# A transformer block on one core: its two inputs also handed over feature-major, and the first loads put in another order

## The chip, the core and the metric

The kernel runs on one core of a Trainium2 chip, in one launch. A core has five engines that work side by side and wait for each other through semaphores: TensorE (PE; its weight loads are listed as PEld), VectorE (DVE), ScalarE (ACT), GpSimd (POOL) and SyncE (SP). SP does nothing but issue DMA transfers here; ACT and POOL can issue them too, each from its own queue, in the order in which the instructions stand on that engine. The metric is the device time of one execution in microseconds (us). The kernel before takes 927.66 us (median of three runs, 927.59 to 928.44).

## What is computed

One block of a hybrid encoder, in float32, for 512 tokens `x` (512 x 1024) and 256 memory tokens `mem` (256 x 1024). Cut to what the change touches:

```python
h = rms_norm(x, g_mix)                      # x * rsqrt(mean(x*x) + eps) * g_mix, row by row
z = h @ w_in                                # every branch reads a part of z
mem_n = rms_norm(mem, mem_g)
kv = mem_n @ w_kv                           # keys: first 512 columns, values: the other 512
# attention of z's query part over k, v; latent attention; mLSTM; gated merge; SwiGLU; final norm
```

The rest of the block (three branches, their gated merge, the output projection, the feed-forward part and the final norm) is some 880 of the 925 us and has the same code before and after.

## The kernel before

**Matmuls in three terms.** A float32 product is made of two parts of each operand: `split` (line 83) writes `hi`, a rounded copy (made by ACT, line 85 or 88), and `lo`, the rest (made by DVE, line 86 or 89). `mm3` (line 101) then issues three matmuls for each pair: hi*hi, hi*lo and lo*hi (lines 104 to 106). So each weight tile costs a load (SP, line 94), one ACT and one DVE pass of 1024 columns (`wload`), and only then matmuls. `raw` has two buffers, `w_hi` and `w_lo` three.

**The head.** TensorE multiplies over features, so it needs `x` and `mem` with features on the partitions, and they arrive with tokens on the partitions. Four stages follow each other, each in one loop:

1. `mem` (two tiles of 128 tokens, four loads of half a tile) is turned by 16 transposes on PE (line 365), and split with the gain `mg_t` from PSUM into `mt_hi`, `mt_lo`.
2. The norm factors: ACT squares each row tile and sums it (lines 372 and 377), DVE makes mean + eps (`n_v`, line 113), POOL the power -0.5 (`n_r`, line 115). `x`'s four tiles are multiplied by their factor in place (line 380 or 382). `mem`'s factor `rm` is applied later.
3. The values: four chunks `c` of `w_vm`, each 12 matmuls of 512 columns into the two banks `vps`, which are scaled with `rm` when they are split into `v_hi`, `v_lo`.
4. The keys, for `h` in 0 to 3: eight transposes of `x` (line 404), split with the gain `gx_t` into two feature tiles of `h_hi`, `h_lo` (lines 88 and 89); then one weight tile of `w_kt` with 24 matmuls of 256 columns into a bank of `pg` (two banks). DVE reads that bank once (`kf`, line 410, times `rbc`, the factors of `mem` as a row), which frees it for the key after the next.

`prepare` (line 263) loads five small constants by SP (line 265) at the end of the head in the code, and POOL zeroes a few tiles. After the head come the tiles of `w_in` (`z_tile`, line 205): 24 matmuls of 512 columns each over all of `h_hi` and `h_lo`; the first two are queries of the memory attention.

**What sets the order.** The code is not run in the order in which it is written. A scheduler in the compiler, with a model of the engines, puts each engine's instructions into one fixed list; a change at the start moves rows in all of it. On the chip each engine then takes its list strictly in order. DMA completions are counted on eight semaphores that SP's and ACT's transfers share in turn, so a transfer is issued only when the eighth transfer before it has landed; that wait stands on the issuing engine, in its list.

**Farther on.** `finish_pair` (line 621) ends a pair of mLSTM heads: four transposes of `hn` (line 633), then `tho` on DVE (line 634) and `ob_hi` on ACT (line 88). `latent_units` (line 696) squares two z tiles on ACT (`csq`, `sq`, line 723), adds them on DVE (line 709) and sums the rows by four small matmuls with `ones` (line 714).

Of the kernel before, what the change touches and what calls it, by code (L numbers as in the profile page):

```python
# [19 lines left out]
P = 128  # L20
S = 512
NT = S // P
D = 1024
KD = D // P
DFF = 2816
NF = DFF // P
MEM = 256
NMT = MEM // P
# [29 lines left out]


@with_exitstack  # L60
def block_kernel(ctx, tc, x, mem, pos, inv, g_mix, mem_g, g_ffn, g_final, g_q, g_kv, gate_bias,
                 g_head, conv_w, w_zt, w_kt, w_vm, w_uq, w_uk, w_uv, w_qk,
                 w_br, w_out, w_fg, w_fu, w_fd, out):
    nc = tc.nc
    mm = nc.tensor.matmul
    V = nc.vector
# [111 lines left out]
    with ExitStack() as mix:  # L178
# [146 lines left out]
        with tc.tile_pool(name="xp", bufs=1) as xp:  # L325
            mt_hi = xp.tile([P, KD, MEM], F32R, name="mt_hi")
            mt_lo = xp.tile([P, KD, MEM], F32R, name="mt_lo")
            gx_t = xp.tile([P, KD], F32, name="gx_t")
            mg_t = xp.tile([P, KD], F32, name="mg_t")

            def load_x(src, t, eng):
                xt = xp.tile([P, D], F32, name="xt", tag="xt", bufs=6)
                eng.dma_start(out=xt, in_=src[t * P:(t + 1) * P, :])
                return xt

            nc.scalar.dma_start(out=mg_t, in_=mem_g)
            nc.scalar.dma_start(out=gx_t, in_=g_mix)
            mxs = [xp.tile([P, D], F32, name="xt", tag="xt", bufs=6) for _ in range(NMT)]

            def load_mem(half):  # L340
                cols = slice(half * 512, (half + 1) * 512)
                for t in range(NMT):
                    nc.sync.dma_start(out=mxs[t][:, cols], in_=mem[t * P:(t + 1) * P, cols])
# [5 lines left out]
            raws, xs, wvs = {}, [], {}  # L349
            load_mem(0)  # L350
            load_mem(1)
            wvs[0] = wload(w_vm[0], pieces=2)
            wvs[1] = wload(w_vm[1])
            load_v(2)
            xs.append(load_x(x, 0, nc.sync))
            load_v(3)
            xs.append(load_x(x, 1, nc.sync))
            xs.append(load_x(x, 2, nc.sync))
            xs.append(load_x(x, 3, nc.sync))
            for k0 in range(0, KD, 2):  # L360
                tp = bank(ptp if k0 % 4 else pg)
                for k in range(2):
                    for t in range(NMT):
                        c0 = k * MEM + t * P
                        nc.tensor.transpose(tp[:, c0:c0 + P], mxs[t][:, (k0 + k) * P:(k0 + k + 1) * P], ident)
                for k in range(2):
                    split(mt_hi[:, k0 + k], mt_lo[:, k0 + k], tp[:, k * MEM:(k + 1) * MEM], scale=mg_t[:, k0 + k:k0 + k + 1])
            rm = xp.tile([P, NMT], F32, name="rm")
            for t in range(NMT):
                junk = xp.tile([P, D], F32, name="junk", tag="junk", bufs=1)  # L370
                ss = xp.tile([P, 1], F32, name="ss", tag="ss", bufs=2)
                A.activation(junk, mxs[t], AF.Square, accum_out=ss)
                V.tensor_copy(rm[:, t:t + 1], rsqrt_mean(xp, ss, 1, D, "n"))
            for t in range(NT):
                junk = xp.tile([P, D], F32, name="junk", tag="junk", bufs=1)
                ss = xp.tile([P, 1], F32, name="ss", tag="ss", bufs=2)
                A.activation(junk, xs[t], AF.Square, accum_out=ss)
                r = rsqrt_mean(xp, ss, 1, D, "n")
                if t % 2:
                    A.activation(xs[t], xs[t], AF.Copy, scale=r)  # L380
                else:
                    V.tensor_scalar(out=xs[t], in0=xs[t], scalar1=r, scalar2=None, op0=ALU.mult)
            vps = [bank(psc) for _ in range(NMT)]
            for c in range(4):
                wh, wl = wvs[c] if c < 2 else wload(w_vm[c], raw=raws[c])
# [5 lines left out]
            rbc = xp.tile([P, MEM], F32, name="rbc")  # L391
            tp = bank(pg)
            for t in range(NMT):
                rb = xp.tile([P, P], F32, name="rb", tag="rb", bufs=2)
                V.tensor_scalar(out=rb, in0=ones, scalar1=rm[:, t:t + 1], scalar2=None, op0=ALU.mult)
                nc.tensor.transpose(tp[:, t * P:(t + 1) * P], rb, ident)
            A.activation(rbc, tp[:, :MEM], AF.Copy)
            for t in range(NMT):
                split(v_hi[:, t], v_lo[:, t], vps[t], scale=rm[:, t:t + 1])
            for h in range(4):  # L400
                for k in (2 * h, 2 * h + 1):
                    tp = bank(ptp)
                    for t in range(NT):
# [4 lines left out]
                gemm_t(ps[:, :MEM], wh, wl, KD, mt_hi, mt_lo)  # L408
                kf = xp.tile([P, MEM], F32, name="kf", tag="kf", bufs=2)
                V.tensor_tensor(out=kf, in0=ps[:, :MEM], in1=rbc, op=ALU.mult)  # L410
                split(k_hi[:, h], k_lo[:, h], kf)
            prepare()

        def gate_chain():
            fp = mq
# [732 lines left out]
```

## Time and profile before

| what | us |
|---|---|
| median of three runs | 927.66 |
| the profiled execution | 925.3 |
| its span, first to last instruction | 923.4 |
| PE busy in the span | 905.1 |
| DVE busy in the span | 636.1 |
| ACT busy in the span | 509.2 |

The profile is of one execution. Times in its rows are from the start of its span; the span lies 1.9 us inside the execution's own time, and that execution was 2.4 us under the median of the timed runs. Busy time of PE is pipelined: a matmul's row lasts longer than the step to the next one, so the steps between starts are what a stream of matmuls costs.

### The profile page before, as it was taken

To read this page: it belongs to the slowest core of one execution; us is meant where nothing else is said; L and a number is where in the kernel's file an instruction comes from. 1 tells how busy PE (TensorE), PEld (TensorE's weight loads), DVE (VectorE), ACT (ScalarE), POOL (GpSimd) and SP (SyncE) were. 2 spreads that over 40 slices of the span, in tenths; PEclk is the share of its full clock that TensorE was granted. 3 is DMA by queue.
4 is the path that set the end of the run, shared out by engine and by line. 5 is a ranking of instruction groups with operands and counts; after the bars stand their busy time and mean duration, and the time that the engine had idled before them with its cause. 6 is when DMAs were issued, how large, how long until landed. Compare 5 with 4: busy or idle time off the path is not lost.

```text
span 923.4 us, 13931 instructions
## 1 busy us (share of the span) xinstructions
PE 905.1 (98%) x5282; PEld 787.7 (85%) x5282; DVE 636.1 (69%) x1088; ACT 509.2 (55%) x896; POOL 85.2 (9%) x139
## 2 busy tenths in 40 slices
PE   7998999999999999999999999999999999999997
PEld 5987787878888788888888879999999999988886
DVE  5768968888684856677553855989898988354323
ACT  8565676686653456677574445545454545244222
POOL 2001002121111101001000500000000000000200
PEclk9999999999999999999999999999999999999999
DMA  7421244434432122121224250423434431365322
GB/s 274 161 75 47 77 133 125 157 121 140 140 111 92 50 86 83 40 87 60 78 69 160 90 191 17 160 93 125 149 115 127 159 115 69 105 225 162 106 76 91
DMA packets 36675, 104.82 MB, mean 114 GB/s; under 512 B 5169, under 2 KB 7537, under 8 KB 36609
## 3 DMA queue, kind: packets, MB, share of 16 engines
q1 hardware_dynamic: 34560, 99.65, 32.4%
q0 software_dynamic: 1184, 3.24, 1.0%
q10 hardware_dynamic: 864, 1.06, 0.3%
q8 instruction: 41, 0.67, 0.3%
q14 instruction: 26, 0.21, 0.1%
HBM read 97.55 MB, written 6.37 MB: 113 GB/s over the span
## 4 chain that ended last, share of the span: by engine, by line
PE 90%; DVE 4%; DMA 2%; ACT 1%; issue 1%; POOL 0%; POOLq 0%; DVEq 0%; SPq 0%; ACTq 0%
PE pg L104 17%; PE pg L106 17%; PE pg L105 17%; PE po L104 7%; PE po L106 7%; PE po L105 7%; PE psc L104 2%; PE psc L105 2%; PE psc L106 2%; PE ptp L818 2%; DVE w_lo L86 1%; PE ppv L588 1%; PE ppv L587 1%; DMA raw<-w_out_d 1%; PE ppv L586 1%
## 5 line engine op out<-in xcount | busy, mean ns | idle before, releaser
L86 DVE TENSOR_TENSOR w_lo<-raw,w_hi 128x1024 fp32r<-128x1024 f32 (+3 forms) x112 | 126.0, 1127 | 92.4 <-ACT w_hi L85 90.7
L104 PE MATMUL pg<-h_hi,w_hi 128*128 128x512 f32 (+1 forms) x476 | 175.2, 369 | 0.8 <-DVE q_lo L89 0.6
L105 PE MATMUL pg<-h_lo,w_hi 128*128 128x512 f32 (+1 forms) x476 | 175.6, 369 | 0.0
L106 PE MATMUL pg<-h_hi,w_lo 128*128 128x512 f32 (+1 forms) x476 | 175.1, 368 | 0.3 <-DVE w_lo L86 0.3
L85 ACT ACTIVATE w_hi<-raw 128x1024 fp32r<-128x1024 f32 (+3 forms) x112 | 107.0, 958 | 104.4 <-PE pg L105 57.2
L104 PEld LDWEIGHTS pg<-h_hi,w_hi 128*128 128x128 f32 x476 | 89.6, 188 | 15.4 <-DVE q_lo L89 0.8
L106 PEld LDWEIGHTS pg<-h_hi,w_lo 128*128 128x128 f32 x476 | 89.5, 188 | 14.8 <-DVE w_lo L86 0.7
L105 PEld LDWEIGHTS pg<-h_lo,w_hi 128*128 128x128 f32 x476 | 89.5, 188 | 13.7
L571 ACT ACTIVATE e<-e,ccol 128x512 f32<-128x512 f32 (+3 forms) x64 | 32.3, 554 | 28.2 <-DMA e<-a_dr 27.6
L1073 DVE TENSOR_REDUCE nm<-psc 128x1 f32<-128x512 f32 (+1 forms) x48 | 27.7, 596 | 19.9 <-PE psc L106 19.5
L576 DVE TENSOR_TENSOR e<-e,psc 128x512 f32<-128x512 f32 (+3 forms) x64 | 29.1, 482 | 17.5 <-POOL e L574 14.6
L1076 ACT ACTIVATE pn<-psc,nm 128x512 f32<-128x512 f32 (+1 forms) x48 | 29.4, 614 | 17.6 <-DVE nm L1073 17.6
L85 ACT ACTIVATE w_hi<-rawab 128x1024 fp32r<-128x1024 f32 x19 | 20.1, 1059 | 29.0 <-PE pg L105 17.4
L574 POOL TENSOR_SCALAR_AFFINE_SELECT e<-e 128x128 f32<-128x128 f32 x64 | 24.0, 384 | 121.5 <-ACT e L571 110.2
L104 PE MATMUL po<-h_hi,w_hi 128*128 128x256 f32 (+1 forms) x116 | 33.8, 291 | 1.4 <-ACT w_hi L85 1.4
L86 DVE TENSOR_TENSOR w_lo<-rawab,w_hi 128x1024 fp32r<-128x1024 f32 x19 | 23.2, 1222 | 16.1 <-ACT w_hi L85 16.0
L1079 ACT ACTIVATE pn<-pn,rs 128x512 f32<-128x512 f32 (+1 forms) x48 | 29.8, 651 | 7.7 <-DVE rs L1078 7.5
L105 PE MATMUL po<-h_lo,w_hi 128*128 128x256 f32 (+1 forms) x116 | 33.7, 290 | 0.0
L106 PE MATMUL po<-h_hi,w_lo 128*128 128x256 f32 (+1 forms) x116 | 33.6, 290 | 0.0
L86 DVE TENSOR_TENSOR s_lo<-e,s_hi 128x640 fp32r<-128x640 f32 x32 | 26.1, 825 | 4.3 <-ACT s_hi L85 2.6
L105 PE MATMUL po<-w_lo,act_hi 128*128 128x512 f32 (+1 forms) x74 | 27.4, 375 | 0.0
L85 ACT ACTIVATE w_hi<-s 128x1024 fp32r<-128x1024 f32 x19 | 20.1, 1059 | 12.9 <-PE pg L105 9.9
(511 smaller groups left out, 2565.3 us busy)
## 6 DMA issues: line engine op xcount, KB each, us to landing
raw<-w_zt_d SPq DMA_DIRECT2D x46, 512.0 KB, 3.4
raw<-w_fd_d SPq DMA_DIRECT2D x22, 512.0 KB, 3.4
e<-a_dr SPq DMA_DIRECT2D x32, 320.0 KB, 3.4
rawab<-w_fg_d SPq DMA_DIRECT2D x19, 512.0 KB, 3.8
rawab<-w_fu_d SPq DMA_DIRECT2D x19, 512.0 KB, 4.7
raw<-w_br_d SPq DMA_DIRECT2D x12, 512.0 KB, 3.5
raw<-w_out_d SPq DMA_DIRECT2D x8, 512.0 KB, 3.6
act_dr<-u SPq DMA_DIRECT2D x16, 256.0 KB, 3.9
```

The costliest lines, as they stand in the source:

```text
L85: A.activation(hi, src, AF.Copy)
L86: V.tensor_tensor(out=lo, in0=src, in1=hi, op=ALU.subtract)
L104: mm(ps, wh, ah, start=start and i == 0, stop=False, skip_group_check=more)
L105: mm(ps, wh, al, start=False, stop=False, skip_group_check=more)
L106: mm(ps, wl, ah, start=False, stop=stop and i == n - 1, skip_group_check=more)
L571: A.activation(e[:, c0:c0 + n], e[:, c0:c0 + n], AF.Exp, bias=ccol[:, j, d, row:row + 1])
L574: nc.gpsimd.affine_select(out=dg, in_=dg, pattern=[[sgn, P]], compare_op=ALU.is_ge, fill=0.0, base=0, channel_multiplier=-sgn)
L576: V.tensor_tensor(out=e[:, c0:c0 + n], in0=e[:, c0:c0 + n], in1=sc[:, t0:t0 + n], op=ALU.mult)
L818: nc.tensor.transpose(tp[:, c * 256 + q * P:c * 256 + (q + 1) * P], pn[q][:, (kt + c) * P:(kt + c + 1) * P], ident)
L1073: nc.vector.tensor_reduce(out=nm, in_=sc, axis=AX.X, op=ALU.max, negate=True)
L1076: nc.scalar.activation(pn, sc, AF.Exp, bias=nm, accum_out=sm)
L1079: nc.scalar.activation(pn, pn, AF.Copy, scale=rs)
```

## The change

The launch hands over two more arrays: `x_t` and `mem_t`, the same numbers with features on the partitions (128 x 8 x 512 and 128 x 8 x 256). `mem_t` is loaded in four pieces of two feature tiles (`mc`) and split from SBUF; `x_t` in four pieces (`xc`). No transposes of `x` and `mem` are left. The row-major `x` and `mem` are still loaded, as whole tiles, for the norm factors alone, and share a ring of six buffers with `x_t`. The factors of `x` are no longer applied to rows: `as_rows` spreads each over a 128 x 128 tile (`rb`, DVE) and transposes that on PE into a bank, and eight new DVE operations (line 397 of the changed kernel) multiply each feature tile by its gain and that bank, in place, before it is split. `mem`'s two factors are made after the values' matmuls instead of before. `prepare` moves to the front, and its five small loads from SP to ACT.

```diff
             for dst, src in ((bias_t, gate_bias), (convw, conv_w), (gh2, g_head), (gq_t, g_q), (gkv_t, g_kv)):
-                nc.sync.dma_start(out=dst, in_=src)
+                nc.scalar.dma_start(out=dst, in_=src)
...
+            prepare()
+
+            def load_mt(k0):
+                mc = xp.tile([P, 2, MEM], F32, name="mc", tag="mc", bufs=4)
+                nc.sync.dma_start(out=mc, in_=mem_t[:, k0:k0 + 2])
+                for k in range(2):
+                    split(mt_hi[:, k0 + k], mt_lo[:, k0 + k], mc[:, k], scale=mg_t[:, k0 + k:k0 + k + 1])
...
+            def load_xt(k0):
+                xc = xp.tile([P, D], F32, name="xc", tag="xt", bufs=6).rearrange("p (k c) -> p k c", k=2)
+                nc.sync.dma_start(out=xc, in_=x_t[:, k0:k0 + 2])
+                return xc
...
+            def as_rows(ps, rs):
+                for t, r in enumerate(rs):
+                    rb = xp.tile([P, P], F32, name="rb", tag="rb", bufs=2)
+                    V.tensor_scalar(out=rb, in0=ones, scalar1=r, scalar2=None, op0=ALU.mult)
+                    nc.tensor.transpose(ps[:, t * P:(t + 1) * P], rb, ident)
...
+            load_mt(0)
             wvs[0] = wload(w_vm[0], pieces=2)
+            load_mt(2)
+            rx = [factor(x, 0)]
             wvs[1] = wload(w_vm[1])
+            load_mt(4)
+            rx.append(factor(x, 1))
             load_v(2)
...
+            load_mt(6)
+            rx.append(factor(x, 2))
+            rx.append(factor(x, 3))
+            xcs = [load_xt(0), load_xt(2)]
...
+            rm = [factor(mem, t) for t in range(NMT)]
+            rbx = bank(ptp)
+            as_rows(rbx, rx)
             for h in range(4):
+                xc = xcs.pop(0)
+                if h < 2:
+                    xcs.append(load_xt(2 * h + 4))
                 for k in (2 * h, 2 * h + 1):
-                    tp = bank(ptp)
-                    for t in range(NT):
-                        nc.tensor.transpose(tp[:, t * P:(t + 1) * P], xs[t][:, k * P:(k + 1) * P], ident)
-                    split(h_hi[:, k], h_lo[:, k], tp, scale=gx_t[:, k:k + 1])
+                    hf = xc[:, k % 2]
+                    V.scalar_tensor_tensor(out=hf, in0=hf, scalar=gx_t[:, k:k + 1], in1=rbx, op0=ALU.mult, op1=ALU.mult)
+                    split(h_hi[:, k], h_lo[:, k], hf)
```

**ACT's list, its start.** The names are the small constants and the parts of `mem`; DMAHW0 to DMAHW7 are the eight semaphores of transfers. Before:

```order
L336 DMA mg_t<-mem_g_d 128x8
L337 DMA gx_t<-g_mix_d 128x8
L88 ACT_TABLE_LOAD [waits DMAHW0_49]
L88 ACTIVATE mt_hi<-pg,mg_t 128x256 [waits PE_49]
L372 ACTIVATE junk,ss<-xt 128x1024 [waits DMAHW4_49,DMAHW1_49]
L88 ACTIVATE mt_hi<-ptp,mg_t 128x256 [waits PE_49]
```

And now:

```order
L330 DMA mg_t<-mem_g_d 128x8
L331 DMA gx_t<-g_mix_d 128x8
L265 DMA bias_t<-gate_bias_d 128x1
L265 DMA convw<-conv_w_d 128x20
L265 DMA gh_94<-g_head_d 128x4 [waits DMAHW1_49]
L265 DMA gq_t<-g_q_d 128x3 [waits DMAHW3_49]
L265 DMA gkv_t<-g_kv_d 128x2 [waits DMAHW5_49]
L88 ACT_TABLE_LOAD
L88 ACTIVATE mt_hi<-mc,mg_t 128x256 [waits DMAHW0_49]
L88 ACTIVATE mt_hi<-mc,mg_t 128x256
L85 ACTIVATE w_hi<-raw 128x512 [waits DMAHW2_49]
L85 ACTIVATE w_hi<-raw 128x512
```

Five DMA issues now stand ahead of ACT's first computing instruction, and the last three of them wait for transfers: semaphore 1 is that of the first `mc`, 3 that of `gx_t`, 5 that of `bias_t`.

**DVE's list, where values end and keys begin** (`w_lo<-raw` are weight tiles, here of `w_vm`, `w_kt` and `z` in turn; `xc` the new in-place products; `kf` the read of a key's bank). Before, from the split of the last chunk of values' weights and of the first key's:

```order
L86 TENSOR_TENSOR w_lo<-raw,w_hi 128x1024 x2
L89 SCALAR_TENSOR_TENSOR v_lo<-psc,rm,v_hi 128x512 x2
L89 SCALAR_TENSOR_TENSOR h_lo<-ptp,gx_t,h_hi 128x512 x2
L86 TENSOR_TENSOR w_lo<-raw,w_hi 128x1024
L410 TENSOR_TENSOR kf<-pg,rbc 128x256
L86 TENSOR_TENSOR w_lo<-raw,w_hi 128x1024
L86 TENSOR_TENSOR k_lo<-kf,k_hi 128x256
L89 SCALAR_TENSOR_TENSOR h_lo<-ptp,gx_t,h_hi 128x512
L410 TENSOR_TENSOR kf<-pg,rbc 128x256
```

And now, from the first of the new products; the first `w_lo` is the last chunk of the values, the next two are keys 0 and 1:

```order
L397 SCALAR_TENSOR_TENSOR xc<-xc,gx_t,ptp 128x512 x4
L86 TENSOR_TENSOR w_lo<-raw,w_hi 128x1024
L86 TENSOR_TENSOR h_lo<-xc,h_hi 128x512
L113 TENSOR_SCALAR n_v<-ss 128x1
L86 TENSOR_TENSOR h_lo<-xc,h_hi 128x512 x2
L86 TENSOR_TENSOR w_lo<-raw,w_hi 128x1024
L86 TENSOR_TENSOR h_lo<-xc,h_hi 128x512
L364 TENSOR_SCALAR rb<-ones,n_r 128x128
L397 SCALAR_TENSOR_TENSOR xc<-xc,gx_t,ptp 128x512 x2
L113 TENSOR_SCALAR n_v<-ss 128x1
L89 SCALAR_TENSOR_TENSOR v_lo<-psc,n_r,v_hi 128x512
L397 SCALAR_TENSOR_TENSOR xc<-xc,gx_t,ptp 128x512 x2
```

These go straight on with:

```order
L86 TENSOR_TENSOR h_lo<-xc,h_hi 128x512
L364 TENSOR_SCALAR rb<-ones,n_r 128x128
L86 TENSOR_TENSOR w_lo<-raw,w_hi 128x1024
L86 TENSOR_TENSOR h_lo<-xc,h_hi 128x512
L89 SCALAR_TENSOR_TENSOR v_lo<-psc,n_r,v_hi 128x512
L86 TENSOR_TENSOR w_lo<-raw,w_hi 128x1024
L86 TENSOR_TENSOR h_lo<-xc,h_hi 128x512 x2
L410 TENSOR_TENSOR kf<-pg,rbc 128x256 x2
L86 TENSOR_TENSOR w_lo<-raw,w_hi 128x1024
```

All eight products and all eight `h_lo` now stand ahead of the first `kf`; before, the first `kf` came after two `h_lo`, and the last two `h_lo` after all the keys. On PE, the first matmul of key 2 waits for DVE (the bank that the first `kf` frees), and the first new product waits for PE: four transposes of `rb`, of which the last two stand behind chunk 2 of the values.

**PE's list, where the last mLSTM pair ends.** Before, 40 matmuls of z tiles of 512 columns stand between the transposes of `hn` and the row sums of `csq`; the rows left out go on in the same threes:

```order
L633 MATMUL ptp<-ident,hn 128x128 x4
L106 MATMUL pg<-h_hi,w_lo 128x512
L104 MATMUL pg<-h_hi,w_hi 128x512
L105 MATMUL pg<-h_lo,w_hi 128x512
...
L714 MATMUL ptp<-ones,csq 128x2 x4
```

And now there are 13 between them:

```order
L632 MATMUL ptp<-ident,hn 128x128 x4
L106 MATMUL pg<-h_hi,w_lo 128x512
L104 MATMUL pg<-h_hi,w_hi 128x512
L105 MATMUL pg<-h_lo,w_hi 128x512
...
L713 MATMUL ptp<-ones,csq 128x2 x4
```

The small matmuls of `csq` have moved toward the transposes of `hn`; PE takes both in this order.

## Rows read from the trace of the kernel before

**Rows 1.** The page's clock line: 40 slices of the span, tenths of full speed.
```profile
PEclk9999999999999999999999999999999999999999
```
**Rows 2.** Busy time by window: PE, PEld, DVE, ACT, POOL (instructions), clock, DMA share, GB/s.
```profile
24.00:44.00 20.00, 20.00 (x148) 18.82 (x148) 16.09 (x24) 11.97 (x18) 0.52 (x1) 1.00 0.55 180
```
**Rows 3.** Timeline of PE in the head: start us, us, engine, line, operation, idle before.
```profile
10.06 1.22 PE L104 MATMUL psc<-w_hi,mt_hi 128*128 128x512 f32 x2 [0.43 <-ACT w_hi L85]
...
23.74 0.37 PE L104 MATMUL pg<-mt_hi,w_hi 128*128 128x256 f32 x1
...
30.10 0.28 PE L106 MATMUL pg<-mt_hi,w_lo 128*128 128x256 f32 x1
...
33.18 0.28 PE L105 MATMUL pg<-mt_lo,w_hi 128*128 128x256 f32 x1
...
37.15 0.40 PE L104 MATMUL pg<-h_hi,w_hi 128*128 128x512 f32 x1
...
48.99 0.39 PE L104 MATMUL ppv<-h_hi,w_hi 128*128 128x512 f32 x1
```
**Rows 4.** Chain that ended last, up to 60 us: start us, us, what.
```profile
11.29 0.43 PE psc L105
...
28.91 0.44 PE ptp L404 x4
```
**Rows 5.** DMA issues up to 100 us: queue, count, KB each, median us to landing.
```profile
mg_t<-mem_g_d ACTq DMA_DIRECT2D x1, 4.0 KB, 2.9
gx_t<-g_mix_d ACTq DMA_DIRECT2D x1, 4.0 KB, 3.8
```
**Rows 6.** Timeline of ACT in the head.
```profile
1.25 0.45 ACTq L337 DMA_DIRECT2D gx_t<-g_mix_d  x1
3.82 1.28 ACT L88 ACT_TABLE_LOAD   x1 [3.82 <-DMA mg_t<-mem_g_d]
...
9.38 1.16 ACT L85 ACTIVATE w_hi<-raw 128x512 fp32r<-128x512 f32 x2
10.41 0.85 ACT L88 ACTIVATE mt_hi<-ptp,mg_t 128x256 fp32r<-128x256 f32 x2
...
19.18 1.05 ACT L377 ACTIVATE junk<-xt 128x1024 f32<-128x1024 f32 x1
```
**Rows 7.** Timeline of POOL: the last of the six norm factors.
```profile
20.58 0.55 POOL L115 TENSOR_TENSOR n_r<-n_v,mhalf 128x1 f32<-128x1 f32 x1 [1.30 <-DVE n_v L113]
```
**Rows 8.** The tile xt: issues of x (ns, first and last start), and landing times.
```profile
L333 SPq DMA_DIRECT2D xt<-x_d x4: 328/490/567, 4.2 to 7.3; - x4
...
DMA to landing us min/median/max: 2.7/6.7/10.4
```
**Rows 9.** Timeline of DVE in the head.
```profile
10.06 0.69 DVE L86 TENSOR_TENSOR w_lo<-raw,w_hi 128x512 fp32r<-128x512 f32 x1
10.67 0.28 DVE L395 TENSOR_SCALAR rb<-ones,rm 128x128 f32<-128x128 f32 x1
...
24.44 1.40 DVE L89 SCALAR_TENSOR_TENSOR v_lo<-psc,rm,v_hi 128x512 fp32r<-128x512 f32 x2
25.76 1.40 DVE L89 SCALAR_TENSOR_TENSOR h_lo<-ptp,gx_t,h_hi 128x512 fp32r<-128x512 f32 x2
27.21 1.22 DVE L86 TENSOR_TENSOR w_lo<-raw,w_hi 128x1024 fp32r<-128x1024 f32 x1
28.35 0.41 DVE L410 TENSOR_TENSOR kf<-pg,rbc 128x256 f32<-128x256 f32 x1
```
**Rows 10.** Timelines of DVE and ACT where the last mLSTM pair ends.
```profile
295.12 0.68 DVE L634 SCALAR_TENSOR_TENSOR tho<-tho,ptp 128x512 f32<-128x512 f32 x1
295.83 0.72 ACT L88 ACTIVATE ob_hi<-tho,gh 128x512 fp32r<-128x512 f32 x1 [2.06 <-DVE tho L634]
```
**Rows 11.** Timeline of PE in the memory attention: its longest wait, and just after.
```profile
78.75 0.39 PE L104 MATMUL psc<-k_hi,q_hi 128*128 128x256 f32 x1 [2.01 <-ACT pn L1076]
...
80.53 0.40 PE L106 MATMUL pg<-h_hi,w_lo 128*128 128x512 f32 x1
```

More of the change, by code (lines that the diff above doesn't have):

```diff
@@ L60, in block_kernel @@
 @with_exitstack
-def block_kernel(ctx, tc, x, mem, pos, inv, g_mix, mem_g, g_ffn, g_final, g_q, g_kv, gate_bias,
+def block_kernel(ctx, tc, x, x_t, mem, mem_t, pos, inv, g_mix, mem_g, g_ffn, g_final, g_q, g_kv, gate_bias,
                  g_head, conv_w, w_zt, w_kt, w_vm, w_uq, w_uk, w_uv, w_qk,
@@ L329, in block_kernel @@
             mg_t = xp.tile([P, KD], F32, name="mg_t")
[L331 to L334, printed above, removed]
             nc.scalar.dma_start(out=mg_t, in_=mem_g)
             nc.scalar.dma_start(out=gx_t, in_=g_mix)
[L338 to L343, printed above, removed]
+            prepare()
[4 more added lines that the diff above has]
+                    split(mt_hi[:, k0 + k], mt_lo[:, k0 + k], mc[:, k], scale=mg_t[:, k0 + k:k0 + k + 1])
             def load_v(c):
@@ L347, in load_v, with load_rows @@
                 nc.sync.dma_start(out=raws[c], in_=w_vm[c])
-            raws, xs, wvs = {}, [], {}
-            load_mem(0)
-            load_mem(1)
+            def load_rows(src, t):
+                xt = xp.tile([P, D], F32, name="xt", tag="xt", bufs=6)
+                nc.sync.dma_start(out=xt, in_=src[t * P:(t + 1) * P, :])
+                return xt
+            def load_xt(k0):
+                xc = xp.tile([P, D], F32, name="xc", tag="xt", bufs=6).rearrange("p (k c) -> p k c", k=2)
+                nc.sync.dma_start(out=xc, in_=x_t[:, k0:k0 + 2])
+                return xc
@@ new lines, in factor @@
+            def factor(src, t):
+                rows = load_rows(src, t)
+                ss = xp.tile([P, 1], F32, name="ss", tag="ss", bufs=2)
+                A.activation(rows, rows, AF.Square, accum_out=ss)
+                return rsqrt_mean(xp, ss, 1, D, f"n{t}")
+            def as_rows(ps, rs):
[3 more added lines that the diff above has]
+                    nc.tensor.transpose(ps[:, t * P:(t + 1) * P], rb, ident)
@@ L352, in block_kernel @@
+            raws, wvs = {}, {}
+            load_mt(0)
             wvs[0] = wload(w_vm[0], pieces=2)
+            load_mt(2)
+            rx = [factor(x, 0)]
             wvs[1] = wload(w_vm[1])
+            load_mt(4)
+            rx.append(factor(x, 1))
             load_v(2)
[L355 to L373, printed above, removed]
-            for t in range(NT):
[L375 to L382, printed above, removed]
+            load_mt(6)
@@ L383, in block_kernel @@
+            rx.append(factor(x, 2))
+            rx.append(factor(x, 3))
+            xcs = [load_xt(0), load_xt(2)]
             vps = [bank(psc) for _ in range(NMT)]
             for c in range(4):
-                wh, wl = wvs[c] if c < 2 else wload(w_vm[c], raw=raws[c])
+                wh, wl = wvs[c] if c < 2 else wload(w_vm[c], raw=raws.get(c))
                 for t in range(NMT):
@@ L390, in block_kernel @@
                         start=c == 0, stop=c == 3)
[L391 to L399, printed above, removed]
+            rm = [factor(mem, t) for t in range(NMT)]
+            rbx = bank(ptp)
+            as_rows(rbx, rx)
             for h in range(4):
+                xc = xcs.pop(0)
+                if h < 2:
+                    xcs.append(load_xt(2 * h + 4))
                 for k in (2 * h, 2 * h + 1):
-                    tp = bank(ptp)
-                    for t in range(NT):
-                        nc.tensor.transpose(tp[:, t * P:(t + 1) * P], xs[t][:, k * P:(k + 1) * P], ident)
-                    split(h_hi[:, k], h_lo[:, k], tp, scale=gx_t[:, k:k + 1])
+                    hf = xc[:, k % 2]
+                    V.scalar_tensor_tensor(out=hf, in0=hf, scalar=gx_t[:, k:k + 1], in1=rbx, op0=ALU.mult, op1=ALU.mult)
+                    split(h_hi[:, k], h_lo[:, k], hf)
                 wh, wl = wload(w_kt[h])
@@ L408, in block_kernel @@
                 gemm_t(ps[:, :MEM], wh, wl, KD, mt_hi, mt_lo)
+                if h == 0:
+                    rbm = bank(ptp)
+                    as_rows(rbm, rm)
+                    rbc = xp.tile([P, MEM], F32, name="rbc")
+                    A.activation(rbc, rbm[:, :MEM], AF.Copy)
+                    for t in range(NMT):
+                        split(v_hi[:, t], v_lo[:, t], vps[t], scale=rm[t])
                 kf = xp.tile([P, MEM], F32, name="kf", tag="kf", bufs=2)
@@ L411, in block_kernel @@
                 split(k_hi[:, h], k_lo[:, h], kf)
-            prepare()
         def gate_chain():
@@ L1125 @@
     arrays = {
-        "x": g["x"][0], "mem": g["mem"][0], "pos": g["positions"][0].reshape(NT, P).T,
+        "x": g["x"][0], "x_t": g["x"][0].T.reshape(KD, P, S).transpose(1, 0, 2),
+        "mem": g["mem"][0], "mem_t": g["mem"][0].T.reshape(KD, P, MEM).transpose(1, 0, 2), "pos": g["positions"][0].reshape(NT, P).T,
         "inv": (f(10000.0) ** (-np.arange(16, dtype=f) / f(16))).astype(f),
```

## The prediction

> **What bounds the kernel now.** I read the page first: PE is busy for 905 of 923 us, the other engines for at most 636, and its clock is at the full level in every slice [rows 1]. The window from 24 to 44 us then says that it never waits in the keys: 20.00 of 20.00 us, DVE 16.09, ACT 11.97 [rows 2]. So today DVE has slack there, but only some 4 us in 20. The timeline of PE cuts the head into pieces [rows 3]: values' matmuls start at 10.06, keys at 23.74, the first tile of `w_in` at 37.15, and at 48.99 the first two of those tiles are done. I judge the change's head by when PE gets through that same work. From the same rows come the prices of a stream: two z tiles are 48 matmuls of 512 columns and two groups of four transposes (0.44 each [rows 4]), so one matmul costs (48.99 - 37.15 - 0.88)/48 = 0.228; 26 steps of 256 columns between 30.10 and 33.18 cost 0.1185 each. At the half clock level a step of 512 columns is 0.43 [rows 4].
>
> **Part 1: transposes.** Sixteen for `mem` go, and 32 for `x`, eight groups of 0.44 = 3.5 us of PE [rows 4]; four single transposes of `rb` come, about 0.4. PE's own bill in the part that was gapless falls by 3.1 us. Whether that is time depends on what feeds PE then.
>
> **Part 2: the start.** `mem`'s transposes lay ahead of 10.06, so their going lets values start earlier only if ACT does. Its list now has five more DMA issues ahead of the table load and of all its computing, three of them behind landings. `gx_t` landed at 1.25 + 3.8 = 5.05, `mg_t` 2.9 after its issue, near 3.7 [rows 5, 6]; the next in the same queue, `bias_t`, should follow by the same 1.3, near 6.35. The fifth issue (0.45, as that of `gx_t` [rows 6]) ends near 6.8, and the table load, at 3.82 today, lasts 1.28 [rows 6], to 8.1. Two `mt_hi` (0.85) and one half of `w_hi` (0.58 of the 1.16 for two) follow, so 9.5 instead of 10.06: a gain of 0.6. The bounds are 8.1 (what ACT needs is hidden behind the queue) and 10.7 (each landing a further 1.2 late). The five loads cost SP nothing anymore.
>
> **Part 3: the factors of x.** Today they are applied to rows before the transposes, the last made at 20.58 + 0.55 = 21.13 [rows 7], where PE still has values to do. Now no part of `h` exists before all four factors stand as a row in a PSUM bank. Two conditions end last. First PE: from 10.06 to 23.74 it did four chunks of values, at first at the half level (0.43 a step [rows 4]), and a few single transposes, some 0.6 by 0.11 each. Less these and 12 x 0.228 for the last chunk, three chunks are 10.3. From 9.5 that is 19.8, and the last two `rb` transposes stand just behind. Second the factor: the last row tile of `x` landed at 7.3 + 10.4 = 17.7 with 5.24 MB of loads up to its end [rows 8]; now 4.72 MB stand up to there, 15.9 by the same rate. From the start of its Square at 19.18 to the factor at 21.13 took 1.95 [rows 6, 7], and `rb` 0.28 [rows 9]: 18.1 to 19.9. I take 20.2 for the first product, with 18.9 and 21.5 as bounds.
>
> **Part 4: DVE becomes the bound.** From the first product to the first read of a key's bank (`kf`), DVE's list holds 26 instructions, and PE can't start key 2 before that read. Their price, by starts that follow each other [rows 9]: eight products and two `v_lo`, ten reads of PSUM of 512 columns, 0.66 each ((25.76 - 24.44)/2) = 6.6; four `w_lo` at 28.35 - 27.21 = 1.14 each = 4.6; eight `h_lo` without PSUM, as the half of `w_lo` at 10.06 to 10.67, 0.61 = 4.9; two `rb` and two `n_v`, at most 0.28 each, 0.7 to 1.1 with small waits. The sum is 16.8. The products are new: 5.3 us on DVE, which no row of before has; I price them as the PSUM reads that they resemble. In the same time PE has chunk 3 (2.7) and keys 0 and 1 (48 x 0.1185 = 5.7), 8.4 together, so it stands still for some 8 us, in pieces, first at the `w_lo` of chunk 3, which stands behind four products. `kf` starts at 20.2 + 16.8 = 37.0 and lasts 0.41 [rows 9]; key 2 starts at 37.4. Keys 2 and 3 take 5.7, the two z tiles 10.95 without transposes: 54.05, against 48.99. **The head loses 5.1 us** (3.5 with the products starting at 18.9 and the small ones at nothing, 6.4 from 21.5). The 3.1 us of Part 1 are in that number: PE saves them and waits longer.
>
> **Part 5: farther on.** The scheduler's list also moved `csq`. The chain from the transposes of `hn` is `tho` on DVE, 0.68, then `ob_hi` on ACT, 0.72 [rows 10], then ACT's square and the sum on DVE, of the same size as these, 0.7 each. Together 2.8, and one `w_lo` of 1.22 may stand ahead on DVE. Before, 40 matmuls (9.1 us) lay beside it; now 13, 2.96 us. That leaves a wait of 0 to 1.3; I take 0.9, since both the `w_lo` and semaphores come on top. In the memory attention PE waited 2.01 at 78.75 on ACT, and 0.6 soon after [rows 11]; the list there is mixed anew, and I leave those waits as they are, with 2.6 below as the bound of the gain. All else I count as nothing: the same matmuls in a stretch where PE waits for little, so a wait that arises would cost its whole length.
>
> **Sum.** 5.1 + 0.9 = +6.0. The profiled execution of 925.3 becomes 931.3; the median shown stands 2.4 above that execution, so 927.66 becomes **933.7**.
>
> **Rivals.** **A, PE stays the bound: faster.** For it speaks that PE has no gap in the keys today and loses 3.1 us of work there [rows 2, 4]. Then 0.6 + 3.1 = 3.7 go: 924.0. It needs the 26 instructions done in the 8.4 us that PE has; the break-even is at 16.8 - 5.1 = 11.7, which leaves 0.45 an instruction, under every row of 512 columns that DVE shows. Chance 0.06.
>
> **B, no difference.** The products start at 18.9 (3.8 lost in the head), `csq` finds its cover, and the new mix takes the 2.6 out of the memory attention [rows 11]: +1.2, 928.9. Each is possible, all three together not likely: 0.11.
>
> **C, the clock falls as well.** Today the only long wait, 2.01 us, left the clock as it was: the matmuls after it last 0.39 and 0.40 us [rows 11], as at 37.15 [rows 3]. The waits of Part 4 come in two pieces of some 3.3 us each, longer than any that the trace has. If keys 2 and 3 then run at the half level, each of the 48 matmuls takes 0.215, half of 0.43 [rows 4], instead of 0.1185: +4.6, 938.3. The Trainium skill, "TensorE: Matmul & The Clock Gate", section "HAM oscillation — how this bites in real kernels", has such a loop: an array that waits for data drops to 1.2 GHz, and then its next work starts cold; by that rule this rival decides, and the trace so far, with 2.01 us and no fall, neither shows nor excludes it. Chance 0.17.
>
> **D, loads come late: the transposes' cost returns as a wait for DMA.** The last weights of the values now stand behind two pieces of `x_t`, 6.3 MB from the start; by the rate of [rows 8] they land at 21.3, and `w_hi` is ready at 22.5, while DVE reaches their `w_lo` at 20.2 + 4 x 0.66 = 22.84. Just in time. Two us later would push the whole chain by 1.7: 935.4. Chance 0.06.
>
> **How the numbers follow.** The forecast itself has 0.60. 0.2% of 927.66, 1.9 us, is about what a measurement here tells from no change. Slower: forecast, C and D, 0.83; same: B, 0.11; faster: A, 0.06. The low end takes in B, 928.5; the high end C with a little of the latent bound, 939.5. Outside stay A and the far ends of C, some 0.15.
>
> **What will show it.** Of the changed kernel: first values matmul at 9.5 (above 10.7: ACT's queue is worse than priced); first product near 20.2; from there DVE without gaps for 17 us and PE with waits that name DVE's `w_lo` and `kf`; key 2 at 37.4; the end of the second z tile at 54; behind the last `hn` a wait of PE for `csq`. Clock below 1.0 in the windows of keys 2 and 3 means C. I am wrong if PE is busy throughout from 20 to 37 us (A), or if DVE waits there for ACT's `h_hi` or for loads, since then the sum of DVE's durations isn't the length of the chain.

## The result and the profile after

The changed kernel takes 940.73 us (median of four runs, 939.62 to 942.47), the kernel before beside it 927.62: a ratio of 1.0137, 95% interval 1.0118 to 1.0156. It is slower, by 13.1 us; forecast were 6.0, and the time lies 1.2 us above the range. The profiled execution took 940.98, close to its median, while that of before lay 2.4 under its own. So the two traces differ by 15.7 us (spans 939.1 and 923.4), and it is these 15.7 that have to be found in them. Of the kernel before, the executions timed beside the experiments lie between 925.1 us, at a mean granted clock of 0.999, and 929.9, at 0.995, and the profiled one (925.3 at 0.999) is among its fastest; so the part behind the head, which the traces below put at 8.4 us, costs 13.1 - 7.25 = 5.9 by the medians.

PE's busy time hardly moved, from 905.1 to 904.8 us; all that was lost is waiting, and matmuls at the half clock level. The page's first part and its clock line, after:

```profile
PE 904.8 (96%) x5238; PEld 788.0 (84%) x5238; DVE 641.8 (68%) x1096; ACT 506.9 (54%) x894; POOL 87.7 (9%) x139
PEclk9898999999999999999999999999999999999999
```

The windows of the changed kernel, with the columns of [rows 2] (the clock stands third from the right), put the stretch that was gapless beside three farther on:

```profile
24.00:44.00 20.00, 16.19 (x97) 14.99 (x98) 17.95 (x29) 12.14 (x21) 3.81 (x2) 0.83 0.44 150
...
84.40:100.00 15.60, 11.42 (x49) 9.25 (x49) 13.20 (x28) 7.64 (x19) 1.03 (x2) 0.78 0.12 35
100.00:163.90 63.90, 63.90 (x309) 51.72 (x307) 47.96 (x79) 40.19 (x80) 5.68 (x15) 1.00 0.35 107
163.90:183.00 19.10, 16.40 (x79) 12.64 (x78) 15.55 (x32) 16.82 (x30) 4.62 (x11) 0.91 0.36 124
```

In [rows 2] PE had 20.00 of 20.00 and a clock of 1.00 there; now DVE is the fuller engine, 17.95, PE has 16.19 at 0.83. The next loss lies at 84.4, where the head is long over.

**The head.** The timeline of PE, the same points as in [rows 3] (start us, us, engine, line, operation, idle before and what ended it):

```profile
10.47 1.23 PE L104 MATMUL psc<-w_hi,mt_hi 128*128 128x512 f32 x2 [10.47 <-ACT w_hi L85]
...
21.47 0.38 PE L365 MATMUL ptp<-ident,rb 128*128 128x128 f32 x2
...
25.80 0.79 PE L105 MATMUL psc<-w_lo,mt_hi 128*128 128x512 f32 x1 [3.24 <-DVE w_lo L86]
...
34.28 0.33 PE L365 MATMUL ptp<-ident,rb 128*128 128x128 f32 x1 [1.20 <-DVE rb L364]
35.42 0.39 PE L106 MATMUL pg<-mt_hi,w_lo 128*128 128x256 f32 x1 [0.81 <-DVE w_lo L86]
...
36.44 0.41 PE L106 MATMUL pg<-mt_hi,w_lo 128*128 128x256 f32 x1
36.65 0.41 PE L104 MATMUL pg<-mt_hi,w_hi 128*128 128x256 f32 x1
...
39.65 0.28 PE L104 MATMUL pg<-mt_hi,w_hi 128*128 128x256 f32 x1
...
45.34 0.40 PE L104 MATMUL pg<-h_hi,w_hi 128*128 128x512 f32 x1
...
56.24 0.39 PE L104 MATMUL ppv<-h_hi,w_hi 128*128 128x512 f32 x1
```

The head ends at 56.24 instead of 48.99: 7.25 of the 15.7 us. Key 1 ran partly at the half level (36.44 to 36.65 is a step of 0.21, against 0.1185). DVE's timeline, first product and first two reads of a key's bank:

```profile
21.89 2.72 DVE L397 SCALAR_TENSOR_TENSOR xc<-xc,gx_t,ptp 128x512 f32<-128x512 f32 x4 [1.28 <-PE ptp L365]
...
38.88 0.41 DVE L410 TENSOR_TENSOR kf<-pg,rbc 128x256 f32<-128x256 f32 x1
39.84 0.42 DVE L410 TENSOR_TENSOR kf<-pg,rbc 128x256 f32<-128x256 f32 x1 [0.55 <-PE pg L106]
```

From the first product to the first `kf` are 38.88 - 21.89 = 17.0 us. The start, on ACT:

```profile
5.86 0.34 ACTq L265 DMA_DIRECT2D gq_t<-g_q_d  x1
7.33 0.33 ACTq L265 DMA_DIRECT2D gkv_t<-g_kv_d  x1
7.70 1.28 ACT L88 ACT_TABLE_LOAD   x1 [7.70 <-DMA gh<-g_head_d]
```

The last of the five issues went at 7.33, and the table load, at 3.82 in [rows 6], at 7.70.

**Behind the head.** From the start of the first `ppv` matmul to the end are 939.1 - 56.24 = 882.9 us, against 923.4 - 48.99 = 874.4: the other 8.4 us. Waits of PE behind the head (engine, line, for whom: us in total, times, longest), after:

```profile
PE psc L104 <- ACT pn L1075: 4.2, 1, 4.2
PE ptp L608 <- ACT nt__1439 L605: 1.9, 1, 1.9
PE po L104 <- DVE x L876: 1.6, 1, 1.6
PE po L104 <- ACT w_hi L85: 1.5, 2, 0.8
PE ptp L713 <- DVE csq L708: 0.8, 1, 0.8
PE psc L565 <- DVE e L575: 0.8, 1, 0.8
PE ptp L752 <- ACT cs L517: 0.6, 1, 0.6
```

The gaps over 0.15 us add up to 12.0 here, and to 6.3 in the same view of before. That is 5.7 of the 8.4. Behind the first two of these waits PE ran at the half level for a while. Of the matmuls of 512 columns, twelve took about 0.43 instead of 0.228, another 2.4 us. Two that follow each other, behind the wait of 4.18:

```profile
88.63 0.58 PE L104 MATMUL psc<-k_hi,q_hi 128*128 128x256 f32 x1 [4.18 <-ACT pn L1075]
...
91.15 0.63 PE L106 MATMUL pg<-h_hi,w_lo 128*128 128x512 f32 x1
91.58 0.63 PE L104 MATMUL pg<-h_hi,w_hi 128*128 128x512 f32 x1
```

In [rows 11] the wait at this place was 2.01. What stands ahead of it on DVE, after: `nm`, which `pn` needs, comes behind seven other instructions, and the first of them waits for a transfer that reads the buffer `brel` (there are two) which it wants to write.

```profile
85.01 1.00 DVE L448 TENSOR_TENSOR_SCAN brel<-t,t 32x256 f32<-32x256 f32 x2 [1.88 <-DMA a_dr<-brel]
85.93 0.46 DVE L450 TENSOR_TENSOR crow<-gi,brel 32x128 f32<-32x128 f32 x2
86.32 0.61 DVE L451 TENSOR_TENSOR brel<-brel,mrow 32x256 f32<-32x256 f32 x2
86.96 0.69 DVE L86 TENSOR_TENSOR om_lo<-ppv,om_hi 128x512 fp32r<-128x512 f32 x1
87.57 0.41 DVE L1072 TENSOR_REDUCE nm<-psc 128x1 f32<-128x256 f32 x1
```

And before, the same place: the same wait, but only three instructions between it and `nm`, 1.4 us instead of 2.6.

```profile
76.30 0.68 DVE L449 TENSOR_TENSOR_SCAN brel<-t,t 32x256 f32<-32x256 f32 x1 [1.51 <-DMA a_dr<-brel]
77.02 0.28 DVE L451 TENSOR_TENSOR crow<-gi,brel 32x128 f32<-32x128 f32 x1
77.22 0.41 DVE L449 TENSOR_TENSOR_SCAN brel<-t,t 32x128 f32<-32x128 f32 x1
77.67 0.43 DVE L1073 TENSOR_REDUCE nm<-psc 128x1 f32<-128x256 f32 x1
```

So two questions: which part of the change makes the head 7.25 us longer, and why does code that wasn't touched take 8.4 us more?

### The profile page after: what moved, and what is told of

Same layout as the page of the kernel before. It is cut to its first block, busy times and chain, and to the rows that moved or that the text cites. A ratio compares the mean times of both kernels' runs of the same rounds, so it can differ in the third digit from the quotient of the medians.

```text
span 939.1 us, 13858 instructions
## 1 busy us (share of the span) xinstructions
PE 904.8 (96%) x5238; PEld 788.0 (84%) x5238; DVE 641.8 (68%) x1096; ACT 506.9 (54%) x894; POOL 87.7 (9%) x139
## 4 chain that ended last, share of the span: by engine, by line
PE 81%; DVE 6%; DMA 5%; ACT 4%; issue 2%; POOL 1%; POOLq 0%; DVEq 0%; SPq 0%; ACTq 0%
PE pg L104 15%; PE pg L105 15%; PE pg L106 15%; PE po L104 7%; PE po L106 7%; PE po L105 7%; DMA e<-a_dr 3%; PE psc L104 2%; PE psc L105 2%; PE psc L106 2%; PE ptp L817 1%; DVE w_lo L86 1%; DMA raw<-w_out_d 1%; ACT e L570 1%; PE ppv L824 1%
## 5 line engine op out<-in xcount | busy, mean ns | idle before, releaser
L86 DVE TENSOR_TENSOR w_lo<-raw,w_hi 128x1024 fp32r<-128x1024 f32 (+3 forms) x113 | 128.0, 1136 | 94.3 <-ACT w_hi L85 92.6
L105 PEld LDWEIGHTS pg<-h_lo,w_hi 128*128 128x128 f32 x476 | 90.1, 189 | 13.7
L85 ACT ACTIVATE w_hi<-rawab 128x1024 fp32r<-128x1024 f32 x19 | 20.1, 1060 | 29.2 <-PE pg L105 16.6
L105 PE MATMUL po<-h_lo,w_hi 128*128 128x256 f32 (+1 forms) x116 | 33.7, 290 | 0.0
```

Of the source, the lines that this page charges most:

```text
L105: mm(ps, wh, al, start=False, stop=False, skip_group_check=more)
```

## The experiments

All runs at a glance. "Behind" is the span minus the end of the head, both from the profiled execution; "list" says whether DVE's list from the end of the keys on is that of the changed kernel (new), that of the kernel before (old), or another one, names of buffers aside. Where it says new or old, the lists of PE and ACT there are the same as well.

| kernel | head ends | list | behind | median us |
|---|---|---|---|---|
| before | 48.99 | old | 874.4 | 927.6 |
| changed | 56.24 | new | 882.9 | 940.7 |
| e1 small loads back | 55.22 | new | 884.5 | 941.7 |
| e2 no product | 54.76 | new | 882.6 | 940.8 |
| e3 product by ones | 55.74 | new | 884.5 | 942.4 |
| e4 `mem_t` alone | 50.99 | new | 885.0 | 935.9 |
| e5 before, `mem`'s factors late | 52.38 | new | 882.9 | 939.1 |
| e6 own buffer | 59.23 | new | 884.4 | 945.3 |
| e7 own buffer, no product | 50.78 | new | 882.7 | 936.5 |
| e8 `mem_t` alone, other order | 50.50 | old | 877.6 | 928.9 |
| e9 changed, other mix | 55.90 | another | 878.6 | 935.1 |
| e10 before, half a step | 48.90 | another, old from mLSTM on | 876.2 | 928.5 |
| e11 changed, four `brel` | 55.47 | another | 879.6 | 937.8 |
| e12 own buffer, by ones | 54.18 | new | 882.4 | 938.9 |

The kernel before ran beside each group at medians of 926.2 to 927.6, single runs from 925.1 to 929.9. A difference of 1 us in "behind" says little; the nine kernels with the new list lie at 882.4 to 885.0, and before and e8, which have the old, at 874.4 and 877.6. Worked out from the medians instead (less the head, and less what the profiled execution has outside its span), the nine lie at 882.6 to 885.1, and before and e8 both near 876.8. In the head a difference of 0.8 us says nothing: the changed kernel, e9 and e11 have the same lists up to the end of the keys, and end the head at 56.24, 55.90 and 55.47.

**e1, the small loads back on SP and at the end.**

```diff
-                nc.scalar.dma_start(out=dst, in_=src)
+                nc.sync.dma_start(out=dst, in_=src)
...
-            prepare()
...
                 split(k_hi[:, h], k_lo[:, h], kf)
+            prepare()
```

> The changed kernel with prepare put back at the end of the head and its five loads back on SP. Theory (ACT's queue holds back the first matmul, but the end of the head hangs on the factors of x and on DVE): first values matmul near 6.5 instead of 10.47; first product near 20.3 instead of 21.89, since the last row tile of x lands no earlier than 16.5 and needs Square, mean and power (about 3.5 in the changed kernel from landing to rb); the head (start of the first ppv matmul) ends 1 to 1.6 us earlier than 56.24. Rival (the queue is the main cost of the head): it ends 3.5 us or more earlier. Second rival (loads set everything): no change within 0.3.

The first matmul came 3.6 us earlier, and the head ended 1.0 earlier, at the low edge of what the theory said:

```profile
6.85 1.22 PE L104 MATMUL psc<-w_hi,mt_hi 128*128 128x512 f32 x2 [6.85 <-ACT w_hi L85]
...
55.22 0.39 PE L104 MATMUL ppv<-h_hi,w_hi 128*128 128x512 f32 x1
```

The first product stood at 19.80, the first `kf` at 36.87: 17.1 us between them again. The delay on ACT's queue is real, but the end of the head hangs on what begins with the first product. The ratio to before is 1.0158 (1.0124 to 1.0192); the time isn't better: the part behind the head took 884.5.

**e2, no product, and e3, a product without the wait.** e2 drops the operation and splits with the gain alone; e3 multiplies by a tile of ones.

```diff
-                    V.scalar_tensor_tensor(out=hf, in0=hf, scalar=gx_t[:, k:k + 1], in1=rbx, op0=ALU.mult, op1=ALU.mult)
-                    split(h_hi[:, k], h_lo[:, k], hf)
+                    split(h_hi[:, k], h_lo[:, k], hf, scale=gx_t[:, k:k + 1])
```

> The changed kernel without the eight products: h is split from x_t with the gain alone, as part of the split (this leaves out the norm factor of x). Takes away 5.3 us of DVE and the wait for the factors. Theory (DVE's list in front of kf is the bound): head ends at 48 to 50 instead of 56.24, and the waits of PE for w_lo in chunk 3 and key 1 go. Rival (late loads or a cold PE are the cause): head still ends above 54.

> The changed kernel with the eight products kept, but by a tile of ones instead of the bank of factors (this leaves out the norm factor of x): the work of DVE stays, the wait for the factors goes. If the length of DVE's work is what costs, the head ends 1.5 to 3 us earlier than 56.24 and well behind the run without products; if the wait for the factors is what costs, it ends within 1 us of the run without products, near 49 to 50.

The head ended at 54.76 and 55.74, hardly earlier. So both theories missed, and in e2 the rival (late loads or a cold PE, above 54) held. DVE's chain, though it is as long as forecast, is not alone: with the products gone, the next thing is almost as late. In e2 PE waited for `w_hi` of a key, and ACT, for the last key, 5.17 us for the load (PE's timeline, then ACT's). Behind PE's wait, key 1 ran at the half level from 33.7 to 36.9 us, which is another 1.5 us:

```profile
31.76 0.39 PE L104 MATMUL pg<-mt_hi,w_hi 128*128 128x256 f32 x1 [1.92 <-ACT w_hi L85]
```
```profile
38.13 1.06 ACT L85 ACTIVATE w_hi<-raw 128x1024 fp32r<-128x1024 f32 x1 [5.17 <-DMA raw<-w_kt_d]
```

The place in the change is one that the prediction passed by: of the values' weights, before, chunks 2 and 3 had buffers of their own, and now chunk 3 goes through the ring `raw` of two. Every key's weights come one place later in that ring, and their loads wait until a `w_lo` frees it: the load for key 1 went at 25.77 us in the changed kernel, when chunk 3's `w_lo` had ended, and at 16.36 before.

**e6 and e7, chunk 3 in a buffer of its own again**, with the product and without; the ring `xt` has five buffers to make room. e12 is e6 with the product by ones.

```diff
+            load_v(3)
             rx.append(factor(x, 2))
```

> The changed kernel with the last values weights loaded into a buffer of their own (as before the change) instead of the ring raw, so that the keys' weights come one place earlier in that ring; the shared ring of row tiles and x_t has five buffers instead of six to make room. If DVE's chain is the bound of the head and loads only come next, the head ends within 1 us of 56.24. If the keys' late loads bind, it ends 2 us or more earlier.

> As the run before this one, and without the eight products (leaves out the norm factor of x). Without products alone the head ended at 54.76, with PE waiting for w_hi of keys 1 and 3 behind late loads. If products and loads bind one behind the other, taking both away ends the head at 49.5 to 52. If neither is the cause, it stays above 54.

> The changed kernel with a buffer of its own for the last values weights, and its products taken with ones instead of the factors (leaves out the norm factor of x): DVE's work stays, the wait for the factors goes. With products and factors and this buffer the head ended at 59.23, without products at 50.78. If the 5 us of DVE are what the products cost, it ends at 55 to 58; if the wait for the factors is, at 50.8 to 53.

e7 came out as expected, 50.78, against 54.76 with the ring. So product and ring bound the head one behind the other: taking the products alone away gains 1.5, giving back the buffer alone nothing, both together 5.5 of the 7.25 us. e6 was a surprise: with the buffer and with the product the head is 3 us later than in the changed kernel. With other loads the scheduler laid the lists out anew: the first product came at 24.28, behind PE's transposes, and PE stood still for 3.58 and 3.46 us in a row:

```profile
36.15 0.47 PE L365 MATMUL ptp<-ident,rb 128*128 128x128 f32 x1 [3.58 <-DVE rb L364]
40.08 0.58 PE L104 MATMUL pg<-mt_hi,w_hi 128*128 128x256 f32 x1 [3.46 <-DVE kf L411]
40.46 0.41 PE L105 MATMUL pg<-mt_lo,w_hi 128*128 128x256 f32 x1
40.67 0.41 PE L106 MATMUL pg<-mt_hi,w_lo 128*128 128x256 f32 x1
```

Then keys 2 and 3 ran at the half level, the window from 40.00 to 48.34 at a clock of 0.66, and took 8.26 us instead of 5.7. That is rival C, at more than half its price, in a kernel other than the one that it was meant for. e12, at 54.18, fell between the two ranges expected: without the wait for the factors the head ends 5.1 earlier than in e6, and without DVE's work too another 3.4 (e7). Both count, the wait more. The kernels compared here differ in the head's lists as well, and e12 too ran a key at the half level, behind a wait of 4.98 us for `kf`, so the shares are rough.

**e4, `mem_t` alone, and e5, only an order of the change.** e4 is the kernel before without `mem`'s transposes, with `mem`'s factors after those of `x`. e5 is the kernel before with one block moved, `mem`'s two norm factors, from ahead of `x`'s four to behind them; the change has this order too:

```diff
-            rm = xp.tile([P, NMT], F32, name="rm")
-            for t in range(NMT):
...
             for t in range(NT):
                 junk = xp.tile([P, D], F32, name="junk", tag="junk", bufs=1)
...
+            rm = xp.tile([P, NMT], F32, name="rm")
+            for t in range(NMT):
...
             vps = [bank(psc) for _ in range(NMT)]
```

> The kernel before with one part of the change: mem_t in place of the 16 transposes of mem; x keeps its transposes, the small loads stay on SP at the end, mem's factors are made after those of x. Theory (the product and its wait made the loss): the head ends at or ahead of the 48.99 of before, 46.5 to 49, and the time is 925 to 929. Rival (PE's transposes were cover, and any change of the list costs some us behind the head): head earlier, but the time over 930.

> The kernel before, computing the same, with one block of its code moved: mem's two norm factors are made after x's four instead of before them. No transposes removed, no x_t, no product. The lists of all engines behind the keys are then, row for row, those of the changed kernel. Theory (half of the loss is the list behind the head, not the head): the time from the start of the first ppv matmul to the end is 882 to 886, as in the five kernels with that list (882.6 to 885.0), against 874.4 of before, with PE's wait of 4.2 us on pn in the memory attention; head end 49 to 52; 933 to 938 in all. Rival (the part behind the head is long because a late or cold head pushes it): 874 to 876 behind the head, the wait near 2 us.

e4: 935.9 us, ratio 1.0095 (1.0067 to 1.0123), with a head only 2.0 later than before. The rest came behind, with the wait of 4.2 us: the rival of that expectation held for the time, though the head wasn't earlier (chunk 3 went through the ring here too). e5 settles it. Its ratio is 1.0124 (1.0105 to 1.0143), without a transpose less or a product more. The head is 3.4 later (52.38, a little outside the expected 49 to 52, as 939.1 in all is of 933 to 938), and behind it stands the changed kernel's wait to 0.02 us:

```profile
52.38 0.39 PE L104 MATMUL ppv<-h_hi,w_hi 128*128 128x512 f32 x1
```
```profile
84.72 0.58 PE L104 MATMUL psc<-k_hi,q_hi 128*128 128x256 f32 x1 [4.16 <-ACT pn L1076]
```

What e5 shares with the changed kernel is not the head's length but the list behind it, and that list takes 882.9 us as there. Nor does a late head push what follows: with the new list, heads that end anywhere from 50.78 to 59.23 are followed by 882.4 to 885.0 us.

What e5 also shares is the order of the factors. In all nine kernels with the new list `mem`'s factors come after `x`'s; in before, e8 and e10 they come first. So this one move, a part of the change, is enough to bring the new list and its loss. Whether the changed kernel with `mem`'s factors put first would get the old list back was not run.

**e8, the reverse: `mem_t` alone, with the old list behind.** Loads and factors in another order, `mem`'s first; the scheduler then laid out the part behind the keys as in the kernel before.

> The kernel before with mem_t in place of mem's 16 transposes, mem's factors ahead of x's, all four values weights with buffers as before, two buffers of pieces of mem_t, loads ordered values first. The engines' lists behind the keys are row for row those of the kernel before. Theory: 874 to 876 behind the head, head end 47 to 50, 922 to 928 in all. Rival (the time behind the head depends on more than the list): over 878 behind the head.

The head was no better than in e4, 50.50 where 47 to 50 was expected, since `x`'s rows now came behind `mem`'s and PE waited for them, 1.6 us. Behind it 877.6, somewhat over the expected 874 to 876, and far below e4's 885.0; the wait on `pn` was 2.0 again. In this trace, unlike in before's, matmuls at the half level follow that wait, some 1.5 us (shown in the last section). In all 928.94, a little over the expected 922 to 928, against 927.36, ratio 1.0014 (1.0002 to 1.0027).

**e9 and e11, the changed kernel with its head as it is and another order behind it.** e9 changes one number in the mixing of the memory attention with the gate chain, e11 gives `brel` four buffers.

```diff
-        run(mem_units(), early, 1.5)
+        run(mem_units(), early, 1.0, 0.0)
```
```diff
-                    brel = fp.tile([P, S], F32, name="brel", tag="brel", bufs=2)
+                    brel = fp.tile([P, S], F32, name="brel", tag="brel", bufs=4)
```

> The changed kernel with one number changed behind the head: the gate chain and the first mLSTM fronts are mixed into the memory attention at one step per step of it instead of 1.5. All computing is the same and the head's lists are the same, row for row; only the order behind it differs. Theory (some 8 us of the loss are the order behind the head): head ends at 56 to 57, the time behind it falls from 882.8 to 870 to 877, PE's wait of 4.2 us in the memory attention goes below 2.5; 927 to 935 in all. Rival (a late head costs behind it whatever the order): still over 880 behind the head.

> The changed kernel with four buffers brel instead of two, so that DVE's scans need not wait for the transfers that read the old ones (1.88 us of waiting at 85.0 in the changed kernel, ahead of the nm that PE's 4.18 us wait hangs on). Theory: that wait of PE falls to 2.5 or less, and the half-level steps after it go; 877 to 881 behind the head. Rival (the order of DVE's list alone is the cause): the wait stays near 4.

e9 needs 878.6 behind a head that ends at 55.90: 4.3 us of the 8.4 between the traces came back by an order alone. By the medians, 935.1 against 940.7, it is nearly all of the 5.9: 5.7, of which 0.3 are the head's. The expected 870 to 877 was too much; new waits arose, 1.6 on `up` and 1.1 on `q_lo`. In e11 the wait on `pn` fell from 4.2 to 2.4 in two pieces, and "behind" to 879.6, as expected:

```profile
PE psc L104 <- ACT pn L1075: 2.4, 2, 1.7
```

That run changed the list as well as the buffers, so it shows that the wait can be had for less, not by which of the two.

**e10, the kernel before, mixed half a step earlier.**

```diff
-        run(mem_units(), early, 1.5)
+        run(mem_units(), early, 1.5, 0.5)
```

> The kernel before with the same mixing started half a step earlier (its ratio stays 1.5). The lists are the same to the end of the keys and again from the mLSTM heads on. Theory: PE's waits of 2.0 and 0.6 us in the memory attention shrink by 1 to 2 us and nothing else moves, 925 to 927; it would beat both kernels. Rival: a new wait takes their place, 927 to 930.

The rival held: PE waits on `crow` instead (1.2), and 1.3 on `nt` farther on. 928.45 against 927.63, ratio 1.0013 (0.9998 to 1.0028). Nothing that was tried beats the kernel before.

## Why the prediction was right and wrong

The direction was right and its mechanism in the head too; the size was wrong, 13.1 instead of 6.0 (15.7 between the traces), chiefly because of Part 5: of the 7.1 us that were missing, 2.2 lie in the head and 4.9 behind it.

**Part 1 (transposes)** held: PE's bill fell by 44 instructions and none of it became time. **Part 2 (the start)** had the right queue and a wrong size. `bias_t` landed at 7.31, not near 6.35, so the fifth issue came at 7.33 and the first matmul at 10.47 instead of 9.5, inside the bounds. Instead of a gain of 0.6 it was a loss of 0.4.

**Part 3 (the first product)** said 20.2, at most 21.5; it was 21.89. The condition was the one named first, PE: the start was 1.0 late, and three chunks took 11.0 us (10.47 to 21.47) instead of 10.3. Most of that is the half level at which the values start in both kernels: it lasted to 13.7 before, where PE had been at `mem`'s transposes from 3.69 on, and to 15.3 here, where nothing ran on PE ahead of 10.47. **Part 4 (DVE's 26 instructions)**: 16.8 forecast, 17.0 measured, 17.1 in e1. The new in-place products took 2.72 for four, 0.66 each beside each other, as the nearest row said. Key 2 began at 39.65, 0.4 behind the end of the first `kf`, as key 1 had run at the half level. Keys 2 and 3 and the z tiles then took 16.6, as forecast. The head lost 7.25 instead of 5.1, and 1.7 of these 2.2 are the late first product.

But Part 4 named this chain as the bound and rival D as a narrow second. The runs showed two bounds at almost the same time: e2 without the products gained only 1.5 us. D had looked at the last weights of the values; what was late were the keys' weights behind them in the ring, and no term had that. In the changed kernel no wait of PE in the head names a load or `w_hi` after the first matmul, since DVE was later still; it matters to whoever would repair it.

**Part 5 is the step that failed.** It read two places in the lists behind the head, priced `csq` at 0.9 (measured: 0.85, of PE waiting for `csq`), left the waits of the memory attention "as they are", and counted "all else" as nothing. That all else was a new list for the engines, up to 359 us of the changed kernel's span: +2.2 in the one wait on `pn`, 2.7 more in other waits besides `csq`, and about 2.4 of half-level matmuls behind them. e5 showed that this loss belongs to the list, not to the head, the products or the transposes: it appears in full where only `mem`'s factors are moved. The range took the memory attention's 2.6 as a possible gain, and nothing there as a possible loss. That was the mistake: where a list is mixed anew, the bound lies on both sides.

**Rivals.** A fell: PE wasn't busy throughout. B fell: nothing vanished. C's own condition did not come about: keys 2 and 3 ran at the full level (16.6 us with the two z tiles, as forecast), so that the time came out near its 938.3 is luck. The clock did fall elsewhere: it read 0.83 in the window from 24 to 44, most of chunk 3 and part of key 1 ran at the half level, mostly under cover of DVE, and so did matmuls behind the head, at the cost above. D fell as stated: the last weights of the values landed at 20.6, not late. The rule that the prediction took from the Trainium skill ("TensorE: Matmul & The Clock Gate", section "HAM oscillation — how this bites in real kernels"), that an array which waits for data starts cold, agrees with e6: 0.66 in keys 2 and 3 behind 3.58 and 3.46 us of waiting. It does not hold for every wait: behind 2.25 us in e7 the keys ran at 1.00.

## What to carry to other kernels

When a compiler's scheduler lays out the whole program, an edit at the start can lay out anew a great deal of what stands behind it; here moving two norm factors did. Compare the two lists all the way, look where the engine that bounds the kernel is served by a long queue of another, and put a loss as well as a gain on it. To tell such a loss from the edit's own, find a version with the old work and the new list (here, one block moved), and one with some of the new work and the old list; and see which small part of the edit goes along with the list. And before calling one chain the bound, ask what the next-latest input would be without it: here a ring that had lost one place stood just behind a chain of DVE work.

## What the runs showed that was not expected

The clock did not follow the length of a single wait. In the kernel before PE waited 2.01 us at 78.75 and 0.61 at 79.97, and the next matmuls of 512 columns took 0.23 a step [rows 11]. In e8, with the same list there, PE waited as long at the same two places, and from 82.03 on six steps took 0.43 each:

```profile
80.21 0.39 PE L104 MATMUL psc<-k_hi,q_hi 128*128 128x256 f32 x1 [2.00 <-ACT pn L1072]
...
81.44 0.80 PE L104 MATMUL pg<-h_hi,w_hi 128*128 128x512 f32 x1 [0.61 <-DVE q_lo L89]
82.03 0.63 PE L105 MATMUL pg<-h_lo,w_hi 128*128 128x512 f32 x1
82.46 0.63 PE L106 MATMUL pg<-h_hi,w_lo 128*128 128x512 f32 x1
```

So the same waits in the same order cost 1.5 us more in one execution than in the other; the runs do not show why. In the changed kernel two waits of 0.83 and 1.86 us lay 2.6 us apart, and the matmuls from 169 to 172 us stepped by 0.43:

```profile
167.57 0.46 PE L608 MATMUL ptp<-ident,nt__1439 66*128 66x66 f32 x4 [1.86 <-ACT nt__1439 L605]
...
169.62 0.63 PE L586 MATMUL ppv<-s_hi,vl 128*64 128x512 f32 x1
170.05 0.63 PE L587 MATMUL ppv<-s_lo,vh 128*66 128x512 f32 x1
```

And five transfers of at most 10 KB at the head of ACT's queue held its first computing instruction until 7.70 us, because each of the last three waited for a transfer ahead of it: with them elsewhere (e1) the first matmul came 3.6 us sooner.
